# Adding squares in pairs on VectorE ahead of the ones-matmuls of a decoder layer, with later norm sums and smaller output transfers in its last stage

## The chip, the cores and the metric

The kernel runs on all 8 cores of one Trainium2 chip, two dies of four cores (cores 0 to 3 and 4 to 7). Each core computes 1024 of the 8192 tokens, alone, with all the weights. The metric is device time in microseconds (us) of the slowest core. TensorE is called PE in the profile, its weight load PEld, VectorE DVE, ScalarE ACT, GpSimd POOL and SyncE SP.

In part of the executions one die gets a lower TensorE clock than the other, and the time is then set by that die. Executions are called slow where this makes over 1 to 1.5%, and are left out of every comparison. But an execution that is still called fast can have a die at a somewhat lower clock, and it is then longer. So besides the timed ratio this document uses a second measure: the mean span of the four cores of a die, taken only from dies whose four cores all had a granted clock of 0.9965 or more. It is called the *clean-die span*; the undisturbed die of an otherwise slow execution counts too. Its readings of one kernel scatter, in one call and between calls. So each run is compared with the kernel before of its own call, and a difference under 1 us is at the limit of what it can tell. The clean-die span lies a few us under the metric, which takes the slowest of eight cores.

## The reference

```python
h = rms_norm(x, norm_mix_pre)
z = h @ w_in                                  # q, k, v, pool input, two gates
...                                           # windowed attention, mean pooling, gated merge
x = x + rms_norm(merged @ w_out, norm_mix_post)
h = rms_norm(x, norm_ffn_pre)
...                                           # GeGLU MLP with causal convolution
ple_gate = sigmoid(rms_norm(x, norm_ple_gate) @ w_ple_gate)
x = x + rms_norm(ple_gate * (p @ w_ple), norm_ple_post)
```

The change touches two places. One is the first `rms_norm`: the sum over 4096 channels of x squared, for each of a core's 1184 tokens (1024 and a halo). The other is the last `rms_norm` with the addition to x and the output.

## The kernel before

Every operation goes through a helper `O(engine, method, reads, writes, ...)`, which records it and works out the semaphore waits. So all instructions have one source line in the profile. Operations of one engine run in the order in which they are recorded.

Stage one goes through the tokens in four slices of 296 (`s`) and each slice in four groups of eight 128-channel blocks (`q`); a group number is `g = 4*s + q`. `prep` squares a group's x on ScalarE (two instructions of four blocks) and scales it on VectorE into `h0`. `stat` adds the squares over channels with matmuls by a matrix of ones. `kv` does the k and v projections of the group. `kv_evac` empties the four PSUM banks of a slice. Three words that come up often: rstd is one over the root of the mean square, the *query job* is the q projection that PE does right after stage one, and a transfer *lands* when the trace records its end.

```python
def prep(g):
    ...
    for hf in range(2):
        t = sq[(2 * g + hf) % 4]
        O("act", "activation", [xt.b], [t.b], out=t.v, in_=xt.v[:, hf*4:(hf+1)*4, :], func=AF.Square)
    for c8 in range(8):
        O("dve", "tensor_scalar", [xt.b, gainB], [h0[c].b], ...)      # h0 = x * gain, bf16
    load_x(g + NXS)                                                   # three x buffers

def stat(g):
    bk = (1 - s % 2) * 4 + 2                     # bank 2 of the OTHER slice's four banks
    for hf in range(2):
        t = sq[(2 * g + hf) % 4]
        for c4 in range(4):
            O("pe", "matmul", [t.b, onesB], [psB[bk]], ..., lhsT=ones_b[:], rhs=t.v[:, c4, :])
    if q == 3:
        ...                                      # rstd of the slice: Ln and Exp on ScalarE

prep(0); prep(1)
for g in range(16):
    s, q = g // 4, g % 4
    if q == 0:
        kv(g, 0, 4); stat(g); kv(g, 4, 8)
    else:
        stat(g); kv(g)
    prep(g + 2)
    if g < 4:
        ...                                      # memset of two key tiles on VectorE
    if g == 3:
        load_const()                             # two loads issued from ScalarE's queue
    if g == 6:
        O("dve", "memset", [], [va.b], ap=va.v..., constant=1.0)      # value tile, 128x5760
    if q == 3:
        kv_evac(s)                               # 10 VectorE multiplies, bank 2 first
```

After stage one the kernel is a stream of matmuls with weights that come through a ring. Other work is kept in a queue of closures (`B.side`), one of which is recorded every so many matmuls (`B.due` counts towards the next). In the last stage the first half of the tokens ends with a norm sum over an f32 accumulator (a matmul with `ones_f`), and the second half is done in two parts of 256 tokens, h = 0 and h = 1:

```python
# end of the first half
B.side.extend(last_A(acc_rstd(acc, ((0, 512),))))
...
# the last gate job of a part
if last:
    B.due = 0
    B.side.extend(last_B(h, last_rstd(h), (t, ap, f)))    # norm sum, rstd, then multiplies and adds
...
# output of four blocks of one part
O("sp", "dma_start", [R.b, tok], [b], dma=f"out{g % 8}", out=out_d[4*g:4*g+4, :, c0:c0+HW]..., in_=R.v)
...
# end of the program, on SP
for e2, k, v in fin:                                      # one wait for each output transfer
    engine.wait_ge(sems[k], val(k, v))
```

The softmax here doesn't subtract the row's maximum and nothing guards it: scores larger than these inputs give would overflow.

Of the kernel before, what the change touches and what calls it, by code (L numbers as in the profile page):

```python
# [13 lines left out]
NCH = 32  # L14
# [321 lines left out]
def build_nc():  # L336
# [29 lines left out]
    with st:  # L366
# [112 lines left out]
        def prep(g):  # L479

            if g >= 4 * NSL:
                return
            s, q = g // 4, g % 4
            xt = xsub[g % NXS]
            for hf in range(2):
                t = sq[(2 * g + hf) % 4]
                O("act", "activation", [xt.b], [t.b], out=t.v, in_=xt.v[:, hf * 4:(hf + 1) * 4, :], func=AF.Square)
            for c8 in range(8):
                c = q * 8 + c8
                O("dve", "tensor_scalar", [xt.b, gainB], [h0[c].b], partial=True, out=h0[c].v[:, s * SL:(s + 1) * SL],  # L490
                  in0=xt.v[:, c8, :], scalar1=gains[:, 0, c:c + 1], scalar2=None, op0=ALU.mult)
            load_x(g + NXS)

        def stat(g):

            s, q = g // 4, g % 4
            bk = (1 - s % 2) * 4 + 2
            for hf in range(2):
                t = sq[(2 * g + hf) % 4]
                for c4 in range(4):  # L500
                    c = q * 8 + hf * 4 + c4
                    O("pe", "matmul", [t.b, onesB], [psB[bk]], partial=c > 0, out=ps[:, bk, 0:SL], lhsT=ones_b[:],
                      rhs=t.v[:, c4, :], start=(c == 0), stop=(c == NCH - 1))
            if q == 3:
                cs = slice(s * SL, (s + 1) * SL)
                O("act", "activation", [psB[bk], onesB], [r0.b], partial=True, out=r0.v[:, cs],
                  in_=ps[:, bk, 0:SL], func=AF.Ln, scale=1.0 / D, bias=epst[:, 0:1])
                O("act", "activation", [r0.b], [r0.b], partial=True, out=r0.v[:, cs], in_=r0.v[:, cs], func=AF.Exp,
                  scale=-0.5)
# [26 lines left out]
        prep(1)  # L536
        for g in range(4 * NSL):
            s, q = g // 4, g % 4
            if q == 0:
                kv(g, 0, 4)  # L540
                stat(g)
                kv(g, 4, 8)
            else:
                stat(g)
                kv(g)
            prep(g + 2)
            if g < 4:
                for t in kz[2 * g:2 * g + 2]:
                    O("dve", "memset", [], [t.b], ap=t.v, constant=0.0)
            if g == 3:  # L550
                load_const()
            if g == 6:
                O("dve", "memset", [], [va.b], ap=va.v.rearrange("p a b -> p (a b)"), constant=1.0)
            if q == 3:
                kv_evac(s)
# [734 lines left out]
        def e_job(hf, f, side):  # L1290
            bg, be = one_bank(512), one_bank(512)

            def evac_g():
                gate(pv(bg), bg[0][0], hf, slice(0, 512), G["sg"][f % 3])

            def evac_e():
                if f == 0:
                    G["acc"] = alloc("acc", [512], F32, hi=True)
                    G["sqf"] = alloc("sqf", [512], F32, hi=True)
                sg = G["sg"][f % 3]  # L1300
                ps_ = r_of(hf, f)
                for t, ap, cols in ps_:
                    O("dve", "tensor_tensor", bufs(be) + [sg.b], [t.b], partial=True, out=ap,
                      in0=ps[:, be[0][0], cols], in1=sg.v[:, cols], op=ALU.mult)
                acc, sqf = G["acc"], G["sqf"]
                d = acc if f == 0 else sqf
                for t, ap, cols in ps_:
                    O("act", "activation", [t.b], [d.b], partial=cols.start > 0, out=d.v[:, cols], in_=ap, func=AF.Square)
                    scale_gain(t, ap, f)
                if f > 0:  # L1310
                    O("dve", "tensor_tensor", [sqf.b, acc.b], [acc.b], out=acc.v, in0=acc.v, in1=sqf.v, op=ALU.add)
                if hf == 0 and f == NCH - 1:
                    B.drain_side()
                    free([h2[0][c] for c in range(NCH)], sqf)
                    B.side.extend(last_A(acc_rstd(acc, ((0, 512),))))
                    B.side.append(reserve)
                    B.side.extend(load_xb(h, g) for h, g in xb_early)

            B.one(B.chunk(bg, NCH, lambda k, h: h2[hf][k].v, lambda k: [h2[hf][k].b], evac_g),
                  B.slabs("b_pg", f, NCH, cast=G["c_pg"][f]), side=side)  # L1320
            B.one(B.chunk(be, 2, lambda k, h: G["pT"][k].v[:, hf * 512:hf * 512 + 512], lambda k: [G["pT"][k].b],
                          evac_e), B.slabs("w_ple", f, 2))

        def half_job(h, f, last, side):

            bg = one_bank(HW)
            be = one_bank(512) if h == 0 else None
            cols = slice(h * HW, (h + 1) * HW)

            def evac():  # L1330
                if f == NCH - NLAST:
                    sum_most(h)
                else:
                    sum_one(h, G["sql"][(f - 1) % 2], False)
                sg = G["sg"][f % 3]
                gate(pv(bg), bg[0][0], 1, cols, sg)
                if last:
                    O("act", "activation", [onesB], [warmB], out=warm, in_=epst[:, 0:1], func=AF.Ln)
                t, ap, _ = r_of(1, f)[h]
                if h == 0:  # L1340
                    O("dve", "tensor_tensor", bufs(be) + [sg.b], [t.b], partial=True, out=ap,
                      in0=ps[:, be[0][0], 0:HW], in1=sg.v[:, 0:HW], op=ALU.mult)
                else:
                    O("dve", "tensor_tensor", [t.b, sg.b], [t.b], partial=True, out=ap, in0=ap, in1=sg.v[:, 0:HW],
                      op=ALU.mult)
                q = G["sql"][f % 2]
                O("act", "activation", [t.b], [q.b], out=q.v, in_=ap, func=AF.Square)
                if last:
                    B.due = 0
                    B.side.extend(last_B(h, last_rstd(h), (t, ap, f)))  # L1350
                else:
                    scale_gain(t, ap, f)

            def evac_e():
                t, ap, c1 = r_of(1, f)[1]
                O("act", "activation", bufs(be), [t.b], partial=True, out=ap, in_=ps[:, be[0][0], c1], func=AF.Copy)

            if h == 0:
                B.one(B.chunk(be, 2, lambda k, h_: G["pT"][k].v[:, 512:1024], lambda k: [G["pT"][k].b], evac_e),
                      B.slabs("w_ple", f, 2))  # L1360
            B.one(B.chunk(bg, NCH, lambda k, h_: h2[1][k].v[:, cols], lambda k: [h2[1][k].b], evac),
                  B.slabs("b_pg", f, NCH, cast=G["c_pg"][f]), side=side)
# [58 lines left out]
        def last_B(h, rstd, lastf):  # L1421
# [5 lines left out]
                scale_gain(*lastf)  # L1427
                rep_rstd(S["r"], HW, 4)

            def put(g):  # L1430
                def run():
                    R = RB[h][g]
                    b = Buf(f"outB{h}{g}")
                    outB.append(b)
                    c0 = 512 + h * HW
                    O("sp", "dma_start", [R.b, tok], [b], dma=f"out{g % 8}",
                      out=out_d[4 * g:4 * g + 4, :, c0:c0 + HW].rearrange("k p t -> p k t"), in_=R.v)
                return run

            def step(g, add):  # L1440
                def run():
                    R, r = RB[h][g], S["r"]
                    if not add:
                        O("dve", "tensor_tensor", [R.b, r.b], [R.b], out=R.v, in0=R.v, in1=r.v, op=ALU.mult)
                        return
                    for i in range(2):
                        x = XB[h][2 * g + i]
                        v = R.v[:, 2 * i:2 * i + 2, :]
                        O("dve", "tensor_tensor", [R.b, x.b], [R.b], partial=i > 0, selfwait=i == 0, out=v, in0=v, in1=x.v,
                          op=ALU.add)  # L1450
                    if h == 1:
                        put(g)()
                    else:
                        free(XB[0][2 * g], XB[0][2 * g + 1])
                        for i in (2 * g, 2 * g + 1):
                            if i + NX < NCH // 2:
                                load_xb(1, i + NX)()
                return run
# [122 lines left out]
```

## Time and profile before

| before | value |
|---|---|
| timed ahead of the change | 6624.95, 6634.72 and 7356.29 us (the last is slow) |
| the profiled execution | 6574.11 us, both dies at clock 0.997 |
| busy: PE, DVE, ACT, POOL | 99%, 31%, 14%, 21% |

The chain that ended last, in shares of the span, on the slowest core (core 5), from the page:

```profile
PE 98%; DMA 1%; DVE 1%; issue 0%; ACT 0%; POOL 0%; DVEq 0%; ACTq 0%; POOLq 0%; SPq 0%
```

PE is the limit nearly everywhere. What PE waited for in the whole span, on core 5 (total us, number of waits, longest):

```profile
PE ps L145 <- DMA sb_arena<-w_in: 30.8, 4, 15.1
PE ps L145 <- DVE sb_arena L145: 13.6, 13, 7.7
PE ps L145 <- ACT sb_arena L145: 5.3, 3, 4.1
PE ps L145 <- DMA sb_wr<-b_pg: 0.3, 1, 0.3
```

Only 50 us of waits are left in 6572. The timeline of core 5 shows the one long wait on VectorE, and how slice three then starts without any (start, us, engine, operation, count, and in brackets the idle time just before):

```profile
63.54 2.13 PE L145 MATMUL ps<-sb_arena,sb_ones_b 128*128 128x296 bf16 x8 [7.71 <-DVE sb_arena L145]
...
80.53 6.20 PE L145 MATMUL ps<-sb_arena 128*128 128x296 bf16 x48
...
84.84 4.67 DVE L145 TENSOR_TENSOR sb_arena<-ps,sb_arena 128x296 bf16<-128x296 f32 x10 [2.16 <-PE ps L145]
86.57 1.17 PE L145 MATMUL ps<-sb_arena,sb_ones_b 128*128 128x296 bf16 x8
```

The first line is slice two's first statistic; it waits for bank 2, which VectorE empties only after it has prepared an x block that lands late. The 48 matmuls at 80.53 are 32 of slice two's last group and 16 of slice three. VectorE's ten evictions at 84.84 begin as soon as PE is through with slice two, and slice three's statistic at 86.57 has no bracket: it didn't wait.

The last stage of core 5, from timelines of PE and of VectorE:

```profile
6301.05 1.10 PE L145 MATMUL ps<-sb_arena,sb_ones_f 128*128 128x512 f32 x2 [2.61 <-DVE sb_arena L145]
...
6514.90 0.27 PE L145 MATMUL ps<-sb_arena,sb_ones_b 128*128 128x256 bf16 x1 [1.04 <-ACT sb_arena L145]
...
6547.50 0.27 PE L145 MATMUL ps<-sb_arena,sb_ones_b 128*128 128x256 bf16 x1 [4.10 <-ACT sb_arena L145]
...
6549.13 0.70 DVE L145 COPY sb_arena<-sb_arena 128x256 f32<-128x256 f32 x3 [0.59 <-ACT sb_arena L145]
6549.93 18.80 DVE L145 TENSOR_TENSOR sb_arena<-sb_arena 128x1024 f32<-128x1024 f32 x24
```

There are three PE waits, at three norm sums, and then 18.8 us of VectorE alone. The last add ends at 6568.73, and 3.7 us later the span ends.

### The profile page before, as it was taken

The numbers are of one execution on the slowest core, as the hardware profiler recorded it, in microseconds if no ns is written. First come the engines' busy times: TensorE is split into PE (matmuls) and PEld (weight loads), VectorE is DVE, ScalarE is ACT, GpSimd is POOL, SyncE is SP. The second block draws the span as 40 slices with busy tenths as digits, with TensorE's granted clock in tenths as the row PEclk, the third lists the DMA queues.
The fourth block names the chain that finished last, engine by engine and source line by source line (L and its number), as shares of the span: only waits on it lengthen the run. The fifth ranks groups of instructions, "written<-read, shape, count | busy, mean of one in ns | idle before, by whom it ended". The sixth has DMA issues, their size and how long they took to land.

```text
span 6572.5 us, 105521 instructions; the slowest of 8 cores (6566.5 to 6572.5 us)
## 1 busy us (share of the span) xinstructions
PE 6497.6 (99%) x41466; PEld 4044.5 (62%) x41466; DVE 2040.5 (31%) x2713; ACT 894.0 (14%) x1397; POOL 1355.0 (21%) x2554
## 2 busy tenths in 40 slices
PE   7999999999999999999999999999999999999998
PEld 5666666666665685866644566665456666544445
DVE  4443111111111236433300133332013333335654
ACT  3640000000001233000000000000000000013433
POOL 1111111111112332211111111111111111233333
PEclk9999999999999999999999999999999999999999
DMA  8568777777776678677799977446774544578888
GB/s 194 83 92 119 117 114 113 119 122 117 116 117 178 178 215 247 144 110 110 110 153 160 152 114 108 77 77 125 160 144 77 77 76 76 129 218 278 240 250 264
DMA packets 387829, 931.69 MB, mean 142 GB/s; under 512 B 50192, under 2 KB 89360, under 8 KB 381584
## 3 DMA queue, kind: packets, MB, share of 16 engines
q0 software_dynamic: 292576, 726.30, 62.2%
q1 hardware_dynamic: 94336, 197.94, 9.2%
q8 instruction: 339, 5.55, 0.3%
q14 instruction: 146, 1.20, 0.1%
q10 hardware_dynamic: 432, 0.70, 0.1%
HBM read 1318.44 MB, written 206.61 MB: 232 GB/s over the span
## 4 chain that ended last, share of the span: by engine, by line
PE 98%; DMA 1%; DVE 1%; issue 0%; ACT 0%; POOL 0%; DVEq 0%; ACTq 0%; POOLq 0%; SPq 0%
PE ps L145 98%; DVE sb_arena L145 1%; DMA sb_arena<-w_in 1%; ACT sb_arena L145 0%; POOL sb_arena L145 0%; DMA sb_wr<-b_pg 0%; DMA sb_arena<-xs 0%; DVEq L144 0%; ACT L145 0%; DVEq L133 0%; ACTq L144 0%; ACT sb_warm L145 0%; POOLq L144 0%; SPq L144 0%; POOLq L170 0%
## 5 line engine op out<-in xcount | busy, mean ns | idle before, releaser
L145 PE MATMUL ps<-sb_arena,sb_wr 128*128 128x512 bf16 (+5 forms) x40000 | 6370.4, 321 | 0.5 <-DMA sb_wr<-b_pg 0.3
L145 PEld LDWEIGHTS ps<-sb_arena,sb_wr 128*128 128x128 bf16 x40000 | 3905.1, 98 | 2381.7 <-issue 7.8
L145 DVE TENSOR_TENSOR sb_arena<-ps,sb_arena 128x512 f32<-128x512 f32 (+12 forms) x936 | 683.9, 733 | 3855.6 <-PE ps L145 3677.0
L145 ACT ACTIVATE sb_arena<-sb_arena 128x512 f32<-128x512 f32 (+11 forms) x727 | 501.8, 693 | 4545.4 <-DVE sb_arena L145 4437.6
L145 DVE TENSOR_TENSOR sb_arena<-sb_arena 128x512 f32<-128x512 f32 (+8 forms) x687 | 545.0, 815 | 512.0 <-ACT sb_arena L145 477.2
L145 POOL DMA_DIRECT2D sb_wr<-w_up x608 | 321.9, 529 | 1748.2 <-PE ps L145 1681.2
L145 DVE SCALAR_TENSOR_TENSOR sb_arena<-sb_arena,sb_cf 128x1024 f32<-128x1024 f32 (+4 forms) x512 | 546.2, 1067 | 40.8 <-DVE sb_arena L145 0.9
L145 POOL DMA_DIRECT2D sb_wr<-w_in x384 | 204.0, 532 | 1242.4 <-PE ps L145 1151.2
L145 POOL DMA_DIRECT2D sb_wr<-w_down x256 | 135.5, 529 | 666.1 <-PE ps L145 639.0
L145 ACT ACTIVATE sb_arena<-ps 128x512 bf16<-128x512 f32 (+8 forms) x299 | 162.8, 545 | 709.9 <-PE ps L145 696.9
L145 PE MATMUL ps<-sb_arena 128*128 128x296 bf16 (+4 forms) x1216 | 180.0, 267 | 33.9 <-DMA sb_arena<-w_in 30.8
L145 POOL DMA_DIRECT2D sb_wr<-b_out x256 | 137.4, 537 | 333.1 <-PE ps L145 309.0
L145 DVE TENSOR_SCALAR sb_arena<-sb_arena,sb_cf 128x1024 f32<-128x1024 f32 (+3 forms) x320 | 183.2, 602 | 59.2 <-DMA sb_arena<-xs 25.7
L145 POOL DMA_DIRECT2D sb_wr<-b_pg x288 | 154.6, 537 | 223.0 <-PE ps L145 195.5
L145 POOL DMA_DIRECT2D sb_wr<-b_down x256 | 137.4, 537 | 273.9 <-PE ps L145 236.6
L145 PEld LDWEIGHTS ps<-sb_arena 128*128 128x128 bf16 (+1 forms) x1216 | 113.6, 98 | 89.7 <-issue 51.0
L145 ACT ACTIVATE sb_arena<-sb_arena,sb_cf 128x512 bf16<-128x512 f32 (+3 forms) x224 | 146.3, 653 | 11.2 <-ACT sb_arena L145 2.0
L145 POOL DMA_DIRECT2D sb_wr<-b_up x160 | 86.1, 538 | 202.4 <-PE ps L145 189.9
L145 ACT ACTIVATE sb_arena<-ps,sb_cf 64x386 f32<-64x386 f32 (+3 forms) x112 | 69.9, 624 | 250.4 <-PE ps L145 247.9
L145 DVE TENSOR_TENSOR sb_arena<-sb_arena,sb_cb 128x512 bf16<-128x512 bf16 (+1 forms) x192 | 64.2, 335 | 45.7 <-ACT sb_arena L145 39.1
L145 POOL DMA_DIRECT2D sb_wr<-w_bp x64 | 33.8, 528 | 190.8 <-PE ps L145 190.8
L145 POOL DMA_DIRECT2D sb_wr<-w_ba x64 | 34.2, 534 | 171.8 <-PE ps L145 171.8
(32 smaller groups left out, 256.3 us busy)
## 6 DMA issues: line engine op xcount, KB each, us to landing
sb_wr<-w_up POOLq DMA_DIRECT2D x608, 256.0 KB, 4.0
sb_wr<-w_in POOLq DMA_DIRECT2D x384, 256.0 KB, 5.6
sb_wr<-b_pg POOLq DMA_DIRECT2D x288, 256.0 KB, 5.0
sb_wr<-b_out POOLq DMA_DIRECT2D x256, 256.0 KB, 3.0
sb_wr<-w_down POOLq DMA_DIRECT2D x192, 256.0 KB, 5.5
sb_wr<-b_down POOLq DMA_DIRECT2D x192, 256.0 KB, 3.7
sb_wr<-b_up POOLq DMA_DIRECT2D x160, 256.0 KB, 3.5
b_out<-w_out POOLq DMA_DIRECT2D x32, 1024.0 KB, 12.3
```

What stands on the lines that cost most here:

```text
L145: inst = getattr(engine, fn[0])(**fn[1])
```

## The change

The intent: halve the ones-matmuls of stage one by adding the squares of a group's two half groups on VectorE first (PE is the limit, VectorE is idle two thirds of the time); let slice one's first statistics go ahead of the weights they don't need; record the norm sums of the last stage later, so that PE doesn't wait for them; and write the last outputs in smaller transfers.

```diff
 def prep(g):
+            a, b = sq[2 * g % 4], sq[(2 * g + 1) % 4]
+            O("dve", "tensor_tensor", [a.b, b.b], [a.b], out=a.v, in0=a.v, in1=b.v, op=ALU.add)
             load_x(g + NXS)
 def stat(g):
-            for hf in range(2):
-                t = sq[(2 * g + hf) % 4]
-                for c4 in range(4):                 # 8 matmuls
+            t = sq[2 * g % 4]
+            for c4 in range(4):                     # 4 matmuls
 ...
-            if q == 0:
+            if q == 0 and s > 0:
                 kv(g, 0, 4)
                 stat(g)
                 kv(g, 4, 8)
 ...
+                    B.side.append(idle)             # ahead of the first half's norm sum
                     B.side.extend(last_A(acc_rstd(acc, ((0, 512),))))
 ...
-                    B.due = 0
+                    B.due = -0.6                    # norm sums of the second half
 ...
-                        put(g)()                    # 512 KB
+                        put(g, 0, 2)()              # 256 KB each
+                        put(g, 2, 2)()
```

## The prediction

> All times are core 5's, the slowest of the profile before (span 6572.5 us, clock 0.997).
>
> **What bounds it.** The chain of waits is PE for 98% of the span. PE's waits sum to only 50 us: 30.8 on the first k/v weights, 13.6 on VectorE (longest 7.7), 5.3 on ScalarE. Only PE's stream, these waits and the tail after the last matmul count.
>
> **Removed: 64 of 128 ones-matmuls of stage one (128x296).** In the timeline 40 matmuls of a group take 5.03 us, 0.126 us each. The Trainium skill, "TensorE: Matmul & The Clock Gate", section "Back-to-back issue gap", gives N/2.4 + 2.5 ns warm, 126 ns here: agreed. Slices two to four lose 48: 6.0 us, plus 0.5 because four of them ran at half clock after a 7.7 us idle. Slice one gains nothing: its last group waits for the last k/v weight (lands at 49.8), and slice two waits for VectorE to empty bank 2, behind an x load that lands at 58.0.
>
> **Added: 16 bf16 adds of 128x1184.** VectorE's bf16 all-SBUF forms took 425 ns for 512 elements and 358 for 384; extrapolated, 0.77 us each (estimate). The skill's "VectorE: DVE Perf Modes", section "Mode 2×_1P", lets bf16 tensor_tensor make two results per cycle; 425 against 687 ns in f32 agrees. They cost in three places:
> - before the eviction that starts slice two, one add: +0.8 us.
> - at slice three: each add makes VectorE wait for ScalarE's squares, which wait for PE's previous statistics. The 4.86 us memset of the value tile starts later, and the eviction behind it. From statistics group 6 on, 12.4 us on VectorE against 10.65 on PE: a new PE wait of about 1.7 us (estimate).
> - two groups later, about 0.4 us.
> Stage one net: -3.5 us (range -6 to 0).
>
> **Last stage.** The first half's norm sum comes one slot (13 matmuls, 2.8 us) later: the 2.61 us PE wait on VectorE at 6301 should vanish. The next sum comes 11 matmuls (1.3 us) later: the 1.04 us PE wait on ScalarE at 6514.9 should vanish. Together -3.6 us. But one more 1.2 us VectorE multiply falls behind the last gate, ahead of the rstd copies that begin the 18.8 us VectorE tail, where VectorE had 0.59 us idle: +0.6 us.
>
> **Outputs in two transfers of 256 KB.** Both are issued after both adds, so only the last landing (3.3 us for 512 KB) can shrink: 0 to -0.5 us.
>
> **Sum:** -3.5 - 3.6 + 0.6 - 0.2 = -6.7 us, 0.1%, less than the spread of the two fast runs before (6625 and 6635). Prediction 6624 us in the fast state, 80% range 6595 to 6645; chances: faster by over 2% 0.01, within 2% 0.98, slower 0.01.
>
> **What would show it right or wrong.**
> - Groups: ones_b 128x296 matmuls x64, not x128; the add near 0.77 us (near 1.25, and the packed mode did not engage).
> - Timeline: slice two's first statistic at about 64.3, not 63.5; a new PE wait of 1 to 2 us on VectorE near 86; first matmul of the query job at about 121.3, not 124.8.
> - PE's waits: the 2.61 and 1.04 us entries gone.
> - End: no idle before VectorE's rstd copies; the stretch from the last weight matmul to the end up to 0.7 us longer.
>
> **What would make it wrong.** Squares of groups 2 and 3 no longer wait behind the first weights, so x buffers come free earlier; if x lands earlier, slice two starts sooner and the gain grows. A longer add, or more evictions behind adds, would eat stage one's gain. A median in the slow state (one run before was 7356) says nothing of the kernel.

## More of the kernel before

The spans of the profiled execution, by die:

```profile
die 0 (median of its cores): 6569.8 us, clock 0.997
die 1 (median of its cores): 6568.9 us, clock 0.997
```

## The result, and the profile after

All results were correct. In the first comparison the changed kernel took 6629.25 us (median of 5, 6626.59 to 6630.69, all fast). The kernel before, in two fast runs, took 6624.95 and 6634.72. The ratio of the fast runs is 0.9998, with a 95% interval of 0.9977 to 1.002. (A ratio is the mean time of one kernel's fast runs over that of the other's fast runs of the same rounds, so it is not quite the ratio of the medians.) The change that the prediction counted on, 6.7 us, is not to be seen in it.

The spans of the changed kernel's profiled execution show why the timed runs can't tell:

```profile
die 0 (median of its cores): 6619.3 us, clock 0.988
die 1 (median of its cores): 6565.0 us, clock 0.997
```

In all five timed executions die 0 had clocks of 0.986 to 0.989 and spans of 6610 to 6629 us, and die 1 had 0.997 and 6561 to 6568. The timed figure measured die 0's clock. The clock records of the profiled execution show how: on die 0 the clock falls to 0.81 in spells of 3.5 to 12 us, 43 of them on cores 0 and 1 and 57 on cores 2 and 3, in all 274 and 366 us. At 0.81 these lose 51 and 69 us (estimate), and these cores' spans are 45 to 64 us longer than die 1's. One spell, on core 2 (stretch, its length, PE busy, granted clock, DMA share, GB/s):

```profile
75.40:83.00 7.60, 7.60 (x53) 0.81 0.98 288
```

For the two timed runs of the kernel before at 6625 and 6635 us no clocks are on record; that they were of the same kind is likely, but not shown. Die 1 alone, against both dies of before, is 4 us shorter. The two traces are therefore compared on the clean cores: 4 to 7 after, all eight before.

The new add and the halved matmuls, from the groups by form on core 5 (count, then busy us and mean ns of one, then idle before):

```profile
L145 PE MATMUL ps<-sb_arena,sb_ones_b 128*128 128x296 bf16 x64 | 12.5, 325 | 22.1 <-DVE sb_arena L145 22.1
L145 DVE TENSOR_TENSOR sb_arena<-sb_arena 128x1184 bf16<-128x1184 bf16 x16 | 12.3, 770 | 16.0 <-ACT sb_arena L145 15.9
```

Half the matmuls are gone, and an add takes 0.770 us, as estimated. But the idle time before the ones-matmuls, which was 7.7 us in this group before, is 22.1 us now. (14.2 us of this is the first statistic of all, which now comes first on PE and waits for the first x block; PE waited just as long for weights before.) The timeline of core 5 at slice three:

```profile
66.97 0.33 ACTq L145 DMA_DIRECT2D sb_cb<-cb  x1
...
67.51 6.59 ACT L145 ACTIVATE sb_arena<-sb_arena 128x1184 bf16<-128x1184 f32 x6 [10.06 <-DVE sb_arena L145]
...
71.05 0.67 PE L145 MATMUL ps<-sb_arena,sb_ones_b 128*128 128x296 bf16 x4
...
75.81 0.76 DVE L145 TENSOR_TENSOR sb_arena<-sb_arena 128x1184 bf16<-128x1184 bf16 x1
76.08 6.20 PE L145 MATMUL ps<-sb_arena 128*128 128x296 bf16 x48
...
77.72 4.86 DVE L145 MEMSET sb_arena<- 128x5760 bf16 x1 [1.15 <-issue]
82.50 2.22 DVE L145 TENSOR_SCALAR sb_arena<-sb_arena,sb_cf 128x296 bf16<-128x296 f32 x8
84.64 0.76 DVE L145 TENSOR_TENSOR sb_arena<-sb_arena 128x1184 bf16<-128x1184 bf16 x1
85.44 4.67 DVE L145 TENSOR_TENSOR sb_arena<-ps,sb_arena 128x296 bf16<-128x296 f32 x10
86.05 0.66 PE L145 MATMUL ps<-sb_arena,sb_ones_b 128*128 128x296 bf16 x4 [3.76 <-DVE sb_arena L145]
86.55 3.36 PE L145 MATMUL ps<-sb_arena 128*128 128x296 bf16 x16
```

Read it from the end. PE is through with slice two's matmuls at 82.3 and waits 3.76 us for the eviction at 85.44. VectorE runs that eviction last in the row: after the add of group 9, which stands after the eight multiplies of group 9, which stand after the memset, which stands after the add of group 8. And VectorE's adds stand behind ScalarE's squares, which started only at 67.51, once the load at 66.97 had left ScalarE's queue. Then the last line: sixteen matmuls take 3.36 us, where sixteen take 2.18 warm. The clock shows why (stretches of 1 us on core 5; PE busy, granted clock, DMA share, GB/s):

```profile
87.00:88.00 1.00, 1.00 (x8) 0.68 1.03 436
88.00:89.00 1.00, 1.00 (x6) 0.50 0.97 407
89.00:90.00 1.00, 1.00 (x6) 0.50 0.27 102
90.00:91.00 1.00, 1.00 (x7) 0.61 0.00 0
```

After the wait the clock went to half, by its records for 3.4 us. These four rows lose 0.32 + 0.50 + 0.50 + 0.39 = 1.7 us. So the new wait costs 3.76 + 1.7 = 5.5 us on this core.

At the first half's norm sum something similar, but in the kernel *before* and to the change's credit. Before, on core 5, after the 2.61 us wait:

```profile
6301.00:6303.00 2.00, 1.95 (x5) 0.80 0.00 0
6303.00:6305.00 2.00, 2.00 (x6) 0.50 0.01 4
6305.00:6307.00 2.00, 2.00 (x9) 0.84 0.46 127
```

That is 2 x (0.20 + 0.50 + 0.16) = 1.7 us lost to the clock after the wait. The clock records show the same 3.4 us at 0.50 on cores 0, 1, 2, 5 and 6; cores 3, 4 and 7 had the same wait and kept full clock. (Cores 0 to 3 also had a spell at 0.81 near 6315, 3.9 to 5.0 us long. It lies in the same stretch and isn't the wait's doing: no core of e7 below, with the same wait, had one.) After the change there is no wait and no half clock there:

```profile
6297.10 1.06 PE L145 MATMUL ps<-sb_arena,sb_ones_f 128*128 128x512 f32 x2
...
6536.10 3.97 DVE L145 TENSOR_TENSOR sb_arena<-sb_arena 128x256 f32<-128x256 f32 x6 [0.68 <-ACT sb_arena L145]
...
6537.89 0.27 PE L145 MATMUL ps<-sb_arena,sb_ones_b 128*128 128x256 bf16 x1 [3.54 <-ACT sb_arena L145]
...
6539.98 0.69 DVE L145 COPY sb_arena<-sb_arena 128x256 f32<-128x256 f32 x3
6540.78 18.80 DVE L145 TENSOR_TENSOR sb_arena<-sb_arena 128x1024 f32<-128x1024 f32 x24
```

The six VectorE instructions at 6536.10 are one more than before, and the copies no longer have an idle time before them, as predicted. The end is the surprise: the last add now ends at 6559.58 and the span at 6564.1, 4.5 us later, against 3.7 before. SP's waits at the end of the program (number, then first and last start), before and after:

```profile
L152 SPq EVENT_SEMAPHORE  x48: 17/17/17, 6569.3 to 6572.2; - x48
```

```profile
L152 SPq EVENT_SEMAPHORE  x56: 17/17/17, 6560.7 to 6563.8; - x56
```

And what held SP's waits up, before (total us, times, longest):

```profile
SPq L152 <- DMA out<-sb_arena: 0.5, 1, 0.5
```

Before, the 48 waits of about 50 ns each were run through when the last transfer landed, and SP waited 0.5 us for it. After, there are 56, they begin 0.55 us later after the last add (one more issue takes 0.47 us), and no such entry is left for these waits. By the trace the last transfer had landed at 6563.0, 0.8 us before the last wait: the row of waits itself ended the program.

The stretches, as means over clean cores (before 8, after 4), from the timelines:

| stretch | before | after | change |
|---|---|---|---|
| slice two's first statistic to the first query matmul | 60.67 | 59.98 | -0.7 |
| first query matmul to the norm sum before the first half's end | 6151.1 | 6150.6 | -0.4 |
| from there to the second half's first norm sum | 206.59 | 202.33 | -4.3 |
| to the second half's second norm sum | 33.55 | 32.35 | -1.2 |
| to the rstd copies | 32.58 | 33.04 | +0.5 |
| to the end | 23.4 | 24.1 | +0.7 |

Of the 4.3 us, 2.8 are what cores 4 and 7 of before, with full clock, show for the wait. The half clock on five of eight cores is another 1.1 on average, and 0.4 are the spells at 0.81 on die 0 of before, which the change had no part in. So the first norm sum brought about 3.9 us.

The 1.04 us wait is gone from its place, but the prediction missed a new one: on all four clean cores PE waits 0.87 us for ScalarE at the next statistic (6511.93 on core 5). It lies in the stretch to the rstd copies, together with a last wait that became shorter (3.54 us on core 5 for 4.10); the stretch as a whole grew by 0.5.

The start of slice two isn't in the table. It comes with the landing of the x block and varies from 58.9 to 65.2 us from core to core, in kernels without the adds alone. So its shift of under 1 us can't be read from one execution.

### The profile page after: what moved, and what is told of

Its sections match the earlier page's. It is cut to its first block, busy times and chain, and to the rows that moved or that the text cites. A ratio compares the mean times of both kernels' runs of the same rounds, so it can differ in the third digit from the quotient of the medians.

```text
span 6629.2 us, 104864 instructions; the slowest of 8 cores (6564.1 to 6629.2 us)
## 1 busy us (share of the span) xinstructions
PE 6528.8 (98%) x40927; PEld 4056.0 (61%) x41402; DVE 2052.1 (31%) x2729; ACT 893.7 (13%) x1397; POOL 1355.2 (20%) x2554
## 4 chain that ended last, share of the span: by engine, by line
PE 97%; DMA 1%; issue 1%; DVE 1%; ACT 0%; POOL 0%; DVEq 0%; ACTq 0%; POOLq 0%; SPq 0%
PE ps L145 97%; DVE sb_arena L145 1%; DMA sb_arena<-w_in 1%; DMA sb_wr<-b_pg 0%; ACT sb_arena L145 0%; POOL sb_arena L145 0%; DMA sb_arena<-xs 0%; DVEq L144 0%; ACT L145 0%; DVEq L133 0%; POOL sb_wr L145 0%; ACTq L144 0%; POOLq L144 0%; SPq L144 0%; POOLq L170 0%
## 5 line engine op out<-in xcount | busy, mean ns | idle before, releaser
L145 DVE TENSOR_TENSOR sb_arena<-sb_arena 128x512 f32<-128x512 f32 (+10 forms) x703 | 557.3, 814 | 529.8 <-ACT sb_arena L145 495.6
```

What stands on the lines that cost most here:

```text
L145: inst = getattr(engine, fn[0])(**fn[1])
```

## The experiments

All are correct kernels, each run beside the kernel before on the same chip. The clean-die spans:

| run | chip | clean-die span (readings) | against before | ratio of fast runs (95%) |
|---|---|---|---|---|
| before | A, first call | 6570.6 (12) | | |
| e1_stage_one | A | 6569.8 (6) | -0.8 | 1.0028 (0.9989 to 1.0068) |
| e2_last_stage | A | 6566.1 (8) | -4.5 | 0.9993 (0.9975 to 1.0011) |
| e3_memset_early | A | 6560.8 (5) | -9.8 | 0.9984 (0.9962 to 1.0005) |
| e4_merged_waits | A | 6565.2 (6) | -5.4 | 0.9991 (0.9969 to 1.0012) |
| before | B | 6569.1 (10) | | |
| e5_change_again | B | 6564.8 (8) | -4.3 | 0.9992 (0.9949 to 1.0035) |
| e6_bank_two_first | B | 6562.2 (10) | -6.9 | 0.9988 (0.9964 to 1.0012) |
| e7_memset_early_in_before | B | 6568.8 (3) | -0.3 | one fast run |
| e8_order_back | B | 6559.5 (9) | -9.6 | 0.9984 (0.9960 to 1.0008) |
| before | A, later call | 6569.4 (15) | | |
| e9_constants_off_scalare | A | 6560.4 (8) | -9.0 | 0.9977 (0.9952 to 1.0002) |
| e10_one_transfer_merged | A | 6563.9 (5) | -5.5 | one fast run |
| e11_simple_best | A | 6559.8 (4) | -9.6 | one fast run |
| e12_all | A | 6559.5 (9) | -9.9 | 0.9976 (0.9951 to 1.0001) |

Not one timed interval excludes 1. Everything that follows rests on the clean-die spans and on stretches of the traces.

### e5: is there an effect at all?

The changed kernel, unedited, on a chip where most executions had both dies at full clock.

> The changed kernel itself, unedited, with the kernel before on the same chip, to size the whole change where both dies are at full clock (0.997); in its first five timed runs one die ran at 0.987 to 0.989. My theory, adding the stretches of the traces: mean core span 3.5 to 6 us under that of before (none of it from stage one, 2.6 + 1.2 from the norm sums, about 1 less in between, minus 0.5 and 0.7 at the end). Rival (the change does nothing, as the ratio 0.9998 of the timed runs says): within 1 us.

Measured: clean-die span 4.3 us under before (8 and 10 readings, deviations 0.6 and 0.5). The timed fast runs say the same: 6568.33 to 6569.44 us (3) against 6573.65 to 6574.79 (3), 5.5 us by their means. The rival falls: the ratio of 0.9998 was the clock of a die, not the kernel. The change is worth 4.3 us, or 0.07%, and the prediction's sum was 6.7.

### e1 and e2: which half of the change brings it?

e1 is the kernel before with the stage-one hunks of the diff alone, e2 with the last-stage hunks alone.

> The kernel before with the stage-one part of the change alone (pair adds, half the ones-matmuls, statistics first in slice one). Read on the cores of the die at full clock: the stretch from slice two's first ones-matmul to the first matmul of the query job; it was 60.3 to 61.3 us before and 59.7 to 60.7 after. My theory (the gain of 6 us is eaten by a new PE wait on VectorE at the start of slice three, made longer by half clock after it): stretch 59.5 to 61, that wait 3.5 to 4.2 us, span as before within 3 us. Rival (the gain is real and was hidden by noise of the DMA landings in slice one): stretch 54 to 57 us, wait under 2 us.

> The kernel before with the last-stage part alone (norm sums one slot and eleven matmuls later, outputs in two transfers). Expected from the two traces: the 2.6 us PE wait at the first half's norm sum gone, 1.0 us saved at the next sum, the stretch from there to the rstd copies 0.5 us longer, and from the copies to the end 0.7 us longer; in sum the span of the cores at full clock 2 to 4 us shorter than before. Rival (all the gain of the whole change on these cores lies in stage one): span as before within 1 us.

Measured: e1 gains 0.8 us, e2 4.5. In e1 the stretch from slice two's first statistic to the query job is 59.9 us on the four clean cores (60.7 before), with a PE wait at slice three of 3.1 to 4.0 us. The line of core 0:

```profile
88.89 0.66 PE L145 MATMUL ps<-sb_arena,sb_ones_b 128*128 128x296 bf16 x4 [3.90 <-DVE sb_arena L145]
```

So my theory holds and the noise theory falls: stage one saves 6 us of matmuls and gives nearly all of it back. (Dies of e1's profiled run had parts at lower clock; only cores 0 to 3 are used.) In e2 all stretches of the last stage are those of the changed kernel to 0.1 us. Its gain lies just above the 2 to 4 us that I expected; the excess is the half clock after the old 2.6 us wait, which I hadn't counted.

The parts add to 5.3 us, the whole to 4.3 in e5. e4, which is the whole with a shorter end, gives 5.4, of which about 0.75 is the end, so 4.6. The sum holds to about 1 us, and I can't resolve more.

### e3 and e7: is it the memset, or the adds?

e3 moves the memset of the value tile in the changed kernel to the start, where VectorE waits for its first inputs. e7 makes the same move in the kernel before.

```diff
+        O("dve", "memset", [], [va.b], ap=va.v..., constant=1.0)
         prep(0)
         prep(1)
 ...
-            if g == 6:
-                O("dve", "memset", [], [va.b], ap=va.v..., constant=1.0)
```

> The changed kernel with one edit: the memset of the value tile (4.86 us on VectorE) comes at the start, when VectorE waits for the first gains, and not in the middle of slice two. My theory (the memset stands between an add that waits for ScalarE and the eviction that PE waits for): the PE wait at slice three falls from 3.8-4.0 us to under 0.7, no half clock after it, and the stretch from slice two's first ones-matmul to the query job falls from about 60 to 54.5-56 us. Rival (the adds themselves keep VectorE late, the memset only happens to lie there): wait stays over 2 us, stretch over 57.5 us.

> Control: the same move of the memset in the kernel before, without the pair adds. If the memset hurts only together with the adds (my theory), nothing changes: stretch from slice two's first ones-matmul to the query job 59.5 to 61.5 us as before. Rival (the memset alone was worth 5 us, the adds have no part in it): stretch about 55.

Measured: in e3 the stretch fell to 54.5 us (mean of 8 cores) and no core had a wait at slice three. The clean-die span fell to 9.8 us under before, 5.2 to 5.5 more than the changed kernel's. That is the wait and its half clock, 3.8 + 1.7 on core 5 of the changed kernel (on the eight cores of e5 the wait is 2.35 to 4.0 us, and three of them kept full clock). In e7 nothing happened: stretch 60.5, span -0.3. So neither the memset nor the adds alone did the harm, but both in one row of VectorE ahead of the eviction. That an add waits for ScalarE before it (2.16 us before the add of group 6 on core 5), and so delays the row, is read from the timeline: no run takes that wait away and leaves the memset in its place. The timeline of e3, core 5:

```profile
80.20 6.20 PE L145 MATMUL ps<-sb_arena 128*128 128x296 bf16 x48
...
83.78 0.78 DVE L145 TENSOR_TENSOR sb_arena<-sb_arena 128x1184 bf16<-128x1184 bf16 x1 [1.24 <-ACT sb_arena L145]
84.59 4.67 DVE L145 TENSOR_TENSOR sb_arena<-ps,sb_arena 128x296 bf16<-128x296 f32 x10
86.25 0.67 PE L145 MATMUL ps<-sb_arena,sb_ones_b 128*128 128x296 bf16 x4
```

VectorE now even has idle time before the last add, and the eviction begins before PE has done the 48 matmuls. The statistic at 86.25 has no bracket.

### e8: does the new order in slice one gain anything?

e3 with `if q == 0:` as before, so the k/v matmuls come first again in slice one.

> The kernel of e3_memset_early with slice one's old order (half a group of k/v matmuls ahead of the first statistics), the pair adds kept. My theory (slice one is bound by the landing of its weights and of the x block, so putting the statistics first gains nothing): start of slice two and of the query job within 1 us of e3 on average (63.7 and 118.2), mean span within 1.5 us of e3. Rival (statistics first frees the x buffers sooner and is worth some us): query job 2 us or more later than in e3.

Measured: -9.6 us against e3's -9.8; slice two starts at 62.3 us on average and the query job at 116.9, against 63.7 and 118.2. That is more than the 1 us that I allowed, in favour of the old order. But the landing of the x block moves both numbers by more than that from core to core, and the spans agree to 0.2 us. Statistics first is worth nothing here, as the prediction said.

### e4 and e10: the end of the program

e4 keeps the two transfers and merges SP's final waits, one for each semaphore with its highest value. e10 does that too, and puts the outputs back into one transfer of 512 KB.

```diff
+        top = {}
+        for eng, k, v in fin:
+            top[eng, k] = max(v, top.get((eng, k), 0))
+        fin = [(eng, k, v) for (eng, k), v in top.items()]
```

> The changed kernel with the waits for outputs at its end merged: one wait for each semaphore (8) instead of one for each transfer (56, about 50 ns each on the queue that also issues the transfers). My theory (after the split the row of 56 waits, begun only after the last issue, ends after the last landing): the end comes 3.1 to 3.5 us after VectorE's last add, against 4.5 in the changed kernel and 3.8 before. Rival (the two last transfers simply land later because the second is issued 0.45 us later): stays at 4.2 to 4.6 us.

> The changed kernel with the outputs of the last part again in one transfer of 512 KB each, and the merged waits of e4. If the split itself is worth nothing, as e4's 3.67 us from VectorE's last add to the end (3.75 before) suggests, this gives 3.6 to 3.8 us too. Rival (the split makes the last landing sooner, and e4 shows that): 4.0 us or more here. Everything else as in the changed kernel; mean span within 0.7 us of e4.

Measured, from VectorE's last add to the end, mean of 8 cores: 3.75 before, 4.51 in the changed kernel (e5), 3.80 in e4, 3.73 in e10. SP's final waits in e4 on core 5:

```profile
L156 SPq EVENT_SEMAPHORE  x8: 17/17/17, 6565.3 to 6567.7; - x8
```

The eight waits span 2.4 us: now they do wait for landings. The rival of e4 falls, as the 0.7 us come back (on six of eight cores in full, on two in part). My range of 3.1 to 3.5 was too hopeful as well: with the waits out of the way the landing takes as long as before. e10 shows that splitting the transfer buys nothing measurable. The split itself was harmless; the longer row of waits, begun one issue later, cost 0.75 us. (e4 keeps the eight extra issues and loses next to nothing by them.)

### e6, e9 and e12: can slice two start earlier?

These three tried to go on from e3. In e6 VectorE empties bank 2 of slice one before it prepares the x block that lands late:

```diff
+            if g == 3:
+                kv_evac(0, (2,))
             prep(g + 2)
 ...
-                kv_evac(s)
+                kv_evac(s, (3, 0, 1) if s == 0 else (2, 3, 0, 1))
```

> The kernel of e3_memset_early with one more edit: at the end of slice one VectorE empties bank 2 before it prepares the x block that lands late, the other three banks after it. My theory (slice two's start waits for the eviction only because it stands behind the x load in VectorE's order): the first ones-matmul of slice two starts at about 56 instead of 61 to 66, a new wait for the second group of statistics of 1 to 5 us follows, and the query job starts at 112 to 115 on average, against 118.2 in e3 (mean of 8 cores); mean span 3 to 6 us under e3's 6560.5. Rival (slice two is bound by the landing of that x block in any case): query job at 117 to 119.

Measured: no gain. The query job starts at 117.9 on average (e3: 118.2) and the span is -6.9, worse than e3's -9.8. Slice two did start sooner, on core 0 at 54.02, but the wait only moved on. The timeline of e6, core 0:

```profile
54.02 0.67 PE L145 MATMUL ps<-sb_arena,sb_ones_b 128*128 128x296 bf16 x4
...
64.56 0.33 ACTq L145 DMA_DIRECT2D sb_cb<-cb  x1
...
65.11 6.80 ACT L145 ACTIVATE sb_arena<-sb_arena 128x1184 bf16<-128x1184 f32 x6 [9.29 <-DVE sb_arena L145]
...
68.40 1.15 PE L145 MATMUL ps<-sb_arena,sb_ones_b 128*128 128x296 bf16 x4 [6.87 <-DVE sb_arena L145]
```

PE waits 6.87 us for group 6's added squares. ScalarE starts them at 65.11, right after a load that it issues at 64.56. That load of constants waits for an earlier one to land, which on this core comes 11 us after its issue (53.59 to 64.49), and holds up ScalarE's instructions behind it. (The bracket on the ACT line names VectorE; the load in front of it in the same queue says otherwise, and e9 tests it.) e9 issues both loads from GpSimd's queue, behind the landing of the same x block:

```diff
-            O("act", "dma_start", [], [constB], partial=True, dma="cst1", ...)
-            O("act", "dma_start", [], [constB], partial=True, dma="cst2", ...)
+            O("pool", "dma_start", [B.cgate], [constB], partial=True, dma="cst1", ...)
+            O("pool", "dma_start", [], [constB], partial=True, dma="cst2", ...)
```

> The kernel of e6 with one more edit: the two loads of constants at the end of slice one are issued from GpSimd's queue (after the landing of the same x block), not from ScalarE's, where the second one waited 10 us for the first to land and held up the squares of group 6. My theory (that queue is what turned e6's earlier start into a wait of 5.6 to 7.6 us for group 6's statistics): the wait falls to 2 to 5 us (VectorE's evictions and memsets then bound it), query job 2 to 4 us earlier than e6's 117.9 on average, mean span 2 to 4 us under e6. Rival (VectorE or the x loads bound it all the same): wait over 5 us, query job within 1 us of e6.

Measured: on core 0 ScalarE squares group 6 at 58.9, and the longest wait of slice two falls from 6.9 to 4.6 us on average. The span is 9.0 under before, 2.1 better than e6, each against before on its own chip. So ScalarE's queue was part of it. The query job, at 116.7, came only 1.2 us sooner, less than I expected: VectorE's nine other evictions and two memsets then stand ahead of group 6.

e12 takes everything together: e9, the nine evictions after group 7, the two memsets at the start, the merged waits of e4, and one side slot per 16 matmuls in the last eight jobs.

> All edits together: those of e11, bank 2 emptied first, its other three banks after the preparation of group 7, the two memsets of key tiles at the end of slice one moved to its start, constants loaded from GpSimd's queue. My theory: PE's waits after slice one's weights add up to under 6 us (in e3: 5.6 to 8.8 before slice two alone), the query job starts at 108 to 114, mean span 14 to 18 us under before. Rival (slice two to four are bound by the landings of the x blocks, about 4 us apart or more, so an earlier start only moves the wait): query job at 115 or later, mean span no better than e11 by more than 2 us.

Measured: -9.9 us, the best of all, but no better than e3 alone within the scatter. The rival's numbers came (the query job starts at 116.2 on average). Its reason, the landings, is only part of what the timeline shows. The waits moved once more. The timeline of e12, core 0:

```profile
68.08 2.36 DVE L149 TENSOR_SCALAR sb_arena<-sb_arena,sb_cf 128x296 bf16<-128x296 f32 x8 [2.73 <-DMA sb_arena<-xs]
...
82.15 0.95 PE L149 MATMUL ps<-sb_arena,sb_ones_b 128*128 128x296 bf16 x4 [3.73 <-DVE sb_arena L149]
```

VectorE now waits for x blocks to land, and the evictions that were put off meet the adds of groups 8 and 9 in front of slice three: 3.8 us of PE wait, on average, are back, and PE's line names VectorE.

### e11: one more slot for the side work

e3 with the merged waits, and 16 for 17 in `half_job(1, f, f == NCH - 1, 17)`.

> The changed kernel with three small edits: memset of the value tile at the start, merged waits, and one more slot for side work in the last eight jobs (one per 16 matmuls, not 17), which should put the extra VectorE multiply back before the last gate. Expected against the changed kernel: 4 us (memset) + 0.8 (waits) + 0.4 to 0.6 (the stretch from the last norm sum to the rstd copies back from 33.05 to about 32.5): mean span 9.5 to 11 us under before. If the 16 only shifts the wait to another place, the stretch stays at 33.

Measured: -9.6 us, at the near end of the range. The merged waits gave back their 0.75 us (23.37 from the copies to the end), but the slot did harm: the stretch to the rstd copies grew from 33.0 to 33.7 us, where 32.5 was hoped for, and the one before it from 32.35 to 32.57. The extra multiply did leave the end. But the wait of the last norm sum on core 5 went back to 4.10 us, as it was before the change, from 3.54. That the finer spacing put VectorE's side work in front of the last gate again is my guess.

## Why the prediction was wrong

The prediction named the right places and got the balance wrong. Term by term, with its own words:

| step of the prediction | predicted | measured |
|---|---|---|
| "Stage one net" | -3.5 | -0.8 (e1) |
| the two norm sums, "Together -3.6 us" | -3.6 | -5.5 (-4.3, of it 0.4 not the change's, and -1.2) |
| "one more 1.2 us VectorE multiply" | +0.6 | +0.5 |
| "Outputs in two transfers of 256 KB" | 0 to -0.5 | +0.75 |
| "Sum" | -6.7 | -4.3 (e5) |

1. **The step that failed first is "a new PE wait of about 1.7 us (estimate)" at slice three.** The wait was there, on the engine and at the time named, but it took 3.8 us on core 5, and 2.35 to 4.0 us on the 32 clean cores of the five profiles that have adds and memset in these places (after, e1, e4, e5, e10). In the prediction's own terms, "12.4 us on VectorE against 10.65 on PE": from the end of statistics 6 (71.55 on core 5) PE's matmuls took 10.7 us, as predicted, and VectorE's side held PE for 14.5 us. So VectorE's side was short by 2.1 us. Most of that is the add of group 8. It ended after 5.0 us, but its squares were done at 74.11, so an add right behind them would have ended after about 3.4 (estimate). VectorE's queue was still full with groups 6 and 7, because ScalarE's squares of group 6 had started late behind a load in its own queue (so the timeline reads; e9 shows that mechanism in a relative of this kernel). The record doesn't list what the 12.4 was made of, so the last half microsecond stays open. e3 and e7 show that the memset in one row with the adds is the cause.
2. **A wait has a second price, which the prediction put only where it had seen it.** It allowed half a microsecond for half clock at slice two, but none after its own new wait (1.7 us lost on core 5). It also overlooked half clock in the profile that it read, after the 2.61 us wait at 6301. So stage one came out worse, and the norm sum better, than the waits alone say. e2 and e3 show both.
3. **The split transfers had the wrong sign.** "Only the last landing ... can shrink" took the landing for the end of the program. SP's row of waits, one for each transfer, was 0.5 us short of being the limit, and eight more waits and eight more issues made it the limit. e4 and e10 show it.
4. **Right:** the add at 0.77 us (0.770 measured), the halved count, no gain from statistics first (e8), the 2.61 us wait gone, 1.2 us gained at the next sum, and six VectorE instructions for five at the end. That this multiply alone makes the +0.5 is not shown: the new 0.87 us wait lies in the same stretch, and e11 took the multiply out of the end without shortening it. The "two groups later, about 0.4 us" was not found as a wait in most cores.
5. **The timed level.** "6624 us in the fast state" took its base from two timed runs of 6625 and 6635 us, while the profiled execution of the same kernel took 6574. That difference of over 50 us, seven times the expected gain, was in plain view and was not asked about. The changed kernel's executions show a die at 0.988 in each of the runs near 6629, and e5 shows both kernels near 6570 with full clocks. That 6629 us fell inside the predicted 6595 to 6645 is luck: it took a session with die 0 at 0.988, and the runs near 6570 fall outside.

As to the Trainium skill: "VectorE: DVE Perf Modes", section "Mode 2×_1P", says that a bf16 tensor_tensor makes two results per cycle; the add of 1184 elements in 0.770 us agrees (an f32 one of 1024 takes 1.22 us in the trace of before). "TensorE: Matmul & The Clock Gate", section "What's actually happening", says that about 3.4 us of idleness bring the clock to half; the 3.76 us wait at slice three agrees, and the point below on the 2.6 us wait does not. It isn't a sharp limit here either: in e12 cores 1 and 7 waited 3.94 us at slice three and kept full clock.

Left open: the 0.5 to 1 us by which the parts and the whole differ; how the cost of an add before slice two (predicted 0.8 us) stands against landings that vary by 5 us from core to core; and what sets off the spells at 0.81 that make a die run at 0.988 in one session and not in another.

## What to carry to other kernels

Work moved to an idle engine isn't free: whatever stands behind it in that engine's order, here a memset and an eviction, inherits its time and its waits, so look at what follows in the same queue and move what can go early out of the way. Count a PE wait of 2.6 us or more, as here, with the half clock that may follow it, and count a program's final row of waits as work. When an effect is a thousandth of the time, look at the clock of each die before believing a timed ratio, and compare stretches of traces between dies at the same clock.

## What the Trainium skill lacked or had wrong

- "TensorE: Matmul & The Clock Gate" ("Why this matters for your kernels") allows PE idle gaps up to about 3 us. In the kernel before, a gap of 2.6 us was followed by clock 0.50 for 3.4 us, so 1.7 us lost, on five of eight cores; three kept full clock. In before, e1 and e7 together, 14 of 20 clean cores lost it after this same gap.
- The same page says that a die with three or more busy cores goes to 13/16 of the clock, stays there while the load lasts, and to budget for it. Here eight cores ran dense matmuls for 6.5 ms at a mean granted clock of 0.997 in most fast executions. The 13/16 itself is in the traces (0.8125, the only value between half and full), but in spells: one of 3.9 to 5.0 us on each core of die 0 in before, 43 or 57 on those in after, one or two of up to 294 us in e1, and none in the other eleven profiles. They differ between pairs of cores of one die. Slow executions had means from 0.98 down to 0.819 on a die.
- No page that I read gives the time of a row of satisfied semaphore waits on one queue: about 50 ns each here, 3.1 us from the first to the last of 56, and it ended the program.
- No page that I read warns that a transfer issued from ScalarE's queue, if it has to wait for another to land, holds up the activations behind it: here for about 10 us, on an engine that the profile shows as idle.
